# Norming the first two strips of attention probabilities on GpSimd instead of VectorE

## The chip, the cores and the metric

The kernel runs on one core of a Trainium2 chip. The metric is the device time of one execution in microseconds; the time of a kernel is the median of its runs. The profile is of one further execution.

## The reference

Two transformer blocks follow each other on 512 tokens of width 1024, in float32. The first has two attentions, then a gated feed-forward layer; the second has three attentions side by side. What the change touches is the softmax in them:

```python
# block 1, branch A: 8 heads, sliding window of 128, bias and sink column
probs = softmax(concat([logits, sink]))[..., :span];  out = probs @ v
# block 1, branch B: 8 heads; compressed, selected and window attention, gated
p_s = softmax(ls);  p_w = softmax(lw)
out = gate0 * (p_c @ v_cmp) + gate1 * (p_s @ v_slc) + gate2 * (p_w @ v_win)
# block 2: MLA, 8 heads of 96; differential, 4 heads of two maps; memory, 4 heads on 256 keys
p = softmax(causal(q @ k.T * scale));  o = p @ v
a = p[0] - lam * p[1];                 o = a @ v
p = softmax(q @ k_mem.T / 8);          o = p @ v_mem
```

With 512 tokens and 16 blocks of 64 to choose, the selected attention takes all earlier keys, so both it and the window are causal attentions over 512 keys with a bias.

## The kernel before

Matrix products are made in three parts: each operand is split into a rounded part H and a rest L, and `mm3` (L299) adds H x H, H x L and L x H in PSUM. Weights come in 1 MB pieces on SP's queue into one of two buffers `raw`; `wsplit` (L132) rounds a piece to `wH` on ScalarE (L136) and subtracts to `wL` (L137) on VectorE, or on GpSimd where a stage sets `leng` so, as the second attention stage does for its filler.

Attention goes by heads through `pipeline` (L269). A head is a unit with a part a (scores, softmax) and a part b (transposes, product with the values). In step i part a of unit i, part b of unit i-1 and a filler of weight matmuls are woven into one program order; the filler is the dense work that comes next. The planner under the kernel then orders each engine's instructions by that program order and by when it expects their operands; each engine works its own list in order.

Part a treats the 512 queries in four blocks of 128, b = 0 to 3, called strips. A causal strip has 128(b+1) keys, so the strips have 128, 256, 384 and 512 columns; in the sliding window they have 130, 258, 258, 258 (two of them for the sink); in the memory heads each has 256. For each strip TensorE makes the scores in PSUM, `strip` (L482) adds the bias and takes the minimum on VectorE, and ScalarE takes the exponential with its sum (L484). When all four sums are there, VectorE inverts them (in the second stage it also multiplies them by the gate, L950), and each strip is multiplied by its column of inverses, in place in the tile `e` (two buffers): the norming. There are four places for it:

- L677 in `swa_a`, sliding window, 8 heads: all four strips on VectorE.
- L1414 in `scale_strips`, called by `nsa_a` (L951; 8 heads, 2 passes each, selected and window) and by `mla_a` (L1643; 8 heads): strips 0 to 2 on VectorE, strip 3 on ScalarE (L1411, mask `SAN` = `SAM` = 8).
- L1808 in `mem_a`, 4 memory heads: all four strips on VectorE.

The differential heads do not norm; L1733 joins their two maps on VectorE.

Part b transposes the normed 128 x 128 blocks on TensorE in `tr_bank` (L493), up to four into one bank of PSUM; a bank is split to `PTH` on ScalarE (L108) and `PTL` on VectorE (L109) and multiplied with the values. In the causal heads the first bank holds one block of each strip, in the memory heads too; in the sliding window it holds blocks of strips 0, 1 and 2.

GpSimd's other work in these stages: in the sliding window the DMA of each head's bias strip (L647), its sink columns (L648) and the rest of a head's output (L627); in the second stage the bias tile (L941, L942), L627 and the filler's `wL` (L137); around the first MLA heads the rotary embedding of the differential queries and keys (L1190, L1211, L1215, L1217); later the gating of outputs (L1614), the DMAs that rearrange the differential queries (L1692, L1693), and once `yL` (L1843).

Of the kernel before, what the change touches and what calls it, by code (L numbers as in the profile page):

```python
# [66 lines left out]
HPQ = 20  # L67
HPF = 0
PGE = 0.9
SPS = 0  # L70
SPN = 0
SPM = 0
SPE = 0
ZG = 0
DP = 0
BS = 0.25
# [9 lines left out]
class Build:  # L86
# [414 lines left out]
    def block1(self):  # L501
# [140 lines left out]
        def swa_a(h):  # L642
# [27 lines left out]
            for b in range(4):  # L670
# [3 lines left out]
                if SAS >> b & 1:  # L674
                    nc.scalar.activation(es, es, AF.Copy, scale=sm[:, b:b + 1])
                    continue
                (nc.gpsimd if b < SPS else nc.vector).tensor_scalar(es, es, sm[:, b:b + 1], None, op0=ALU.mult)  # L677
            state[h] = blk
# [257 lines left out]
        def nsa_a(h, br):  # L936
# [13 lines left out]
            nc.vector.tensor_tensor(sm, sm, gate[:, :, 3 * h + 1 + br], op=ALU.mult)  # L950
            self.scale_strips(e, sm, SPN, SAN)  # L951
            yield
# [472 lines left out]
    def block2(self, out):  # L1425
# [211 lines left out]
        def mla_a(h):  # L1637
# [4 lines left out]
            v.reciprocal(sm, sm)  # L1642
            self.scale_strips(e, sm, SPM, SAM)  # L1643
            yield
# [144 lines left out]
        def mem_a(h):  # L1789
# [16 lines left out]
            for b in range(4):  # L1806
                es = e[:, 256 * b:256 * b + 256]
                (nc.gpsimd if b < SPE else v).tensor_scalar(es, es, sm[:, b:b + 1], None, op0=ALU.mult)  # L1808
            state["m", h] = e
# [158 lines left out]
```

## Time and profile before

| | |
|---|---|
| median of 3 runs | 1077.21 us (1074.77 to 1085.18) |
| the profiled execution's own time | 1086.88 us, its span 1084.9 us |
| TensorE busy | 1040.1 us, 96% of the span |
| VectorE busy | 751.1 us, 69% |
| ScalarE busy | 581.4 us, 54% |
| GpSimd busy | 233.2 us, 21% |
| sliding window attention | about 80 to 165 us of the span |
| selected and window attention | about 198 to 345 us |
| MLA, then differential and memory heads | about 900 to 972 and 972 to 1045 us |

In the rows PE is TensorE's matmuls, PEld its weight loads, DVE VectorE, ACT ScalarE, POOL GpSimd; L1414 is line 1414 of the kernel. `out<-in` names tiles, `128x256 f32` is partitions by elements. The profile's engine intervals are times in work: waits between instructions are not counted, but an instruction held up while it runs shows a longer duration. The ends of matmuls are modelled. PEclk is the clock granted to TensorE as a share of 2.4 GHz.

### The profile page before, as it was taken

Reading aid. Unit: us, or ns where it says so; the run is one execution under the profiler, and the core shown is the slowest. Engines: PE = TensorE matmul, PEld = TensorE weight load, DVE = VectorE, ACT = ScalarE, POOL = GpSimd, SP = SyncE. Lnnn points to the kernel's source line nnn. Section 1 sums busy time; section 2 is a strip of 40 time slices with the busy share of each in tenths; the row PEclk is TensorE's granted clock in tenths of the full one; section 3 lists DMA queues with packets and bytes.
Section 4 is the critical chain, followed back from the end, with each engine's and each line's share of the span. In section 5 each row is a group of like instructions: output and inputs, shape, how many; then the busy total and the mean of one; then the engine's idle time right before and its main releaser. Section 6 shows DMA issues by size and latency. Waiting matters only on the chain.

```text
span 1084.9 us, 15448 instructions
## 1 busy us (share of the span) xinstructions
PE 1040.1 (96%) x5425; PEld 873.7 (81%) x5425; DVE 751.1 (69%) x1603; ACT 581.4 (54%) x1127; POOL 233.2 (21%) x369
## 2 busy tenths in 40 slices
PE   5899898999999999999999999999999999999898
PEld 3797676878778888888887888887889997877798
DVE  6559885387783275678885468988533497979982
ACT  6447764567784244345553445545643535867630
POOL 4321223322212029000000210000340128230200
PEclk9989998999999999999999999999999999999899
DMA  6936435310233253245669877878855662266442
GB/s 187 278 96 187 107 78 126 83 44 10 45 83 77 72 169 118 78 132 170 205 207 321 289 254 216 256 231 266 292 191 165 226 206 79 79 187 192 141 161 79
DMA packets 131981, 173.09 MB, mean 160 GB/s; under 512 B 8676, under 2 KB 101578, under 8 KB 130752
## 3 DMA queue, kind: packets, MB, share of 16 engines
q1 hardware_dynamic: 127904, 161.47, 48.3%
q0 software_dynamic: 4000, 10.64, 3.2%
q8 instruction: 43, 0.70, 0.3%
q14 instruction: 34, 0.28, 0.1%
HBM read 131.95 MB, written 42.23 MB: 161 GB/s over the span
## 4 chain that ended last, share of the span: by engine, by line
PE 74%; DVE 12%; DMA 6%; ACT 4%; issue 3%; SPq 0%; POOL 0%; POOLq 0%; ACTq 0%; DVEq 0%
PE ps_mm L301 19%; PE ps_mm L306 19%; PE ps_mm L305 18%; DMA raw<-in_w_in 4%; PE ps_S L1361 3%; PE ps_T L493 2%; DVE wL L137 2%; PE ps_O L1390 1%; PE ps_O L1392 1%; DVE PTL L109 1%; PE ps_S L306 1%; PE ps_S L301 1%; PE ps_S L305 1%; ACT wH L136 1%; ACT e L484 1%
## 5 line engine op out<-in xcount | busy, mean ns | idle before, releaser
L136 ACT ACTIVATE wH<-raw 128x1024 fp32r<-128x1024 f32 (+4 forms) x145 | 137.2, 947 | 206.5 <-PE ps_mm L305 159.0
L137 DVE TENSOR_TENSOR wL<-raw,wH 128x1024 fp32r<-128x1024 f32 (+4 forms) x130 | 145.6, 1121 | 98.0 <-ACT wH L136 97.5
L301 PE MATMUL ps_mm<-nH,wH 128*128 128x512 f32 x416 | 162.7, 391 | 0.6 <-DVE qL L115 0.6
L306 PE MATMUL ps_mm<-nH,wL 128*128 128x512 f32 x416 | 162.5, 391 | 0.0
L305 PE MATMUL ps_mm<-nL,wH 128*128 128x512 f32 x416 | 162.4, 390 | 0.0
L484 ACT ACTIVATE e<-e,mn 128x256 f32<-128x256 f32 (+5 forms) x160 | 86.3, 541 | 26.7 <-DVE mn L482 25.5
L301 PE MATMUL ps_mm<-hH,wH 128*128 128x512 f32 x232 | 95.3, 411 | 0.0
L306 PE MATMUL ps_mm<-hH,wL 128*128 128x512 f32 x232 | 92.8, 400 | 0.0
L305 PE MATMUL ps_mm<-hL,wH 128*128 128x512 f32 x232 | 92.7, 400 | 0.0
L301 PEld LDWEIGHTS ps_mm<-nH,wH 128*128 128x128 f32 x416 | 78.1, 188 | 16.6 <-DVE qL L115 0.8
L305 PEld LDWEIGHTS ps_mm<-nL,wH 128*128 128x128 f32 x416 | 78.2, 188 | 15.7
L306 PEld LDWEIGHTS ps_mm<-nH,wL 128*128 128x128 f32 x416 | 78.1, 188 | 15.6
L108 ACT ACTIVATE PTH<-ps_T 128x512 fp32r<-128x512 f32 (+1 forms) x108 | 55.7, 528 | 34.2 <-PE ps_T L493 33.5
L109 DVE TENSOR_TENSOR PTL<-ps_T,PTH 128x512 fp32r<-128x512 f32 (+1 forms) x108 | 63.7, 606 | 12.9 <-ACT PTH L108 10.9
L301 PE MATMUL ps_mm<-aH,wH 128*128 128x512 f32 x176 | 69.6, 396 | 1.1 <-ACT aH L108 1.1
L493 PE MATMUL ps_T<-ident,e 128*128 128x128 f32 x368 | 63.8, 281 | 6.2 <-DVE e L1733 3.1
L305 PE MATMUL ps_mm<-aL,wH 128*128 128x512 f32 x176 | 69.6, 395 | 0.0
L306 PE MATMUL ps_mm<-aH,wL 128*128 128x512 f32 x176 | 69.5, 395 | 0.0
L493 PEld LDWEIGHTS ps_T<-ident,e 128*128 128x128 f32 x368 | 45.6, 143 | 22.6 <-DVE e L1733 4.1
L1075 POOL MEMSET cv<- 128x2 f32 x44 | 4.2, 99 | 236.2 <-DVE cc L1079 229.7
L306 PEld LDWEIGHTS ps_mm<-hH,wL 128*128 128x128 f32 x232 | 44.7, 193 | 9.3 <-DVE wL L137 0.2
L482 DVE CUSTOM_DVE_ANT_0 e<-ps_S,G 128x128 f32<-128x128 f32 (+1 forms) x64 | 30.7, 486 | 29.4 <-PE ps_S L1361 29.0
(585 smaller groups left out, 2624.9 us busy)
## 6 DMA issues: line engine op xcount, KB each, us to landing
raw<-in_w_ffn_in SPq DMA_DIRECT2D x20, 1024.0 KB, 6.1
raw<-in_w_in SPq DMA_DIRECT2D x12, 1024.0 KB, 7.3
pre<-in_w_in SPq DMA_DIRECT2D x17, 512.0 KB, 6.2
raw<-in_w_ffn_out SPq DMA_DIRECT2D x8, 768.0 KB, 5.6
raw<-in_w_ffn_out SPq DMA_DIRECT2D x8, 640.0 KB, 6.1
xt<-in_x SPq DMA_DIRECT2D x8, 512.0 KB, 5.2
raw<-in_w_out SPq DMA_DIRECT2D x4, 1024.0 KB, 5.5
pre_z<-preH SPq DMA_DIRECT2D x16, 256.0 KB, 5.2
```

The source lines that it names most:

```text
L108: nc.scalar.activation(H, src, AF.Copy)
L109: nc.vector.tensor_sub(L, src, f32(H))
L136: self.nc.scalar.activation(H, raw, AF.Copy)
L137: self.leng.tensor_sub(L, raw, f32(H))
L301: ins = mm(ps, wH, xH, start=first, stop=False)
L305: mm(ps, wH, xL, start=False, stop=False)
L306: mm(ps, wL, xH, start=False, stop=last)
L482: nc.vector.tensor_tensor_reduce(e, ps, bias, op0=ALU.add, op1=ALU.min, scale=1.0, scalar=3e38, accum_out=mn)
L484: nc.scalar.activation(e, e, AF.Exp, scale=-1.0, bias=mn, accum_out=sm)
L493: nc.tensor.transpose(ps[:, 128 * i:128 * i + 128], blk, self.ident)
L1361: nc.tensor.matmul(ps[:, :n], q[:, 128 * b:128 * b + 128], k[:, :n], start=i == 0, stop=i == len(prods) - 1)
L1390: mm(out, v2(kb), H[:, c], start=first, stop=False)
```

## The change

`b < SPS` and its like choose GpSimd for strip b; all four limits go from 0 to 2. The multiplications of strips 0 and 1 of every normed head, 72 of them, are then issued on GpSimd, with the same operands. Nothing else is edited.

```diff
-SPS = 0
-SPN = 0
-SPM = 0
-SPE = 0
+SPS = 2
+SPN = 2
+SPM = 2
+SPE = 2
```

The lines that read them (unchanged):

```python
# swa_a
(nc.gpsimd if b < SPS else nc.vector).tensor_scalar(es, es, sm[:, b:b + 1], None, op0=ALU.mult)
# scale_strips(e, sm, pool, sa): pool is SPN in nsa_a, SPM in mla_a
(self.nc.gpsimd if b < pool else self.nc.vector).tensor_scalar(es, es, sm[:, b:b + 1], None, op0=ALU.mult)
# mem_a
(nc.gpsimd if b < SPE else v).tensor_scalar(es, es, sm[:, b:b + 1], None, op0=ALU.mult)
```

## Rows read from the trace of the kernel before

**Rows 1.** The page, busy us by engine (share of the span) and instructions.

```profile
PE 1040.1 (96%) x5425; PEld 873.7 (81%) x5425; DVE 751.1 (69%) x1603; ACT 581.4 (54%) x1127; POOL 233.2 (21%) x369
```

**Rows 2.** Windows of the four stages: length, busy us PE PEld DVE ACT POOL, PEclk, DMA.

```profile
80.00:165.00 85.00, 77.81 (x453) 64.00 (x452) 74.25 (x185) 59.86 (x130) 18.85 (x23) 0.98 0.43 120
198.00:345.00 147.00, 142.57 (x762) 117.34 (x761) 102.92 (x295) 100.17 (x233) 40.35 (x43) 0.99 0.21 50
900.00:972.00 72.00, 67.52 (x398) 56.03 (x397) 59.17 (x153) 52.50 (x127) 34.90 (x55) 0.98 0.34 113
972.00:1045.00 73.00, 68.73 (x408) 58.12 (x407) 67.87 (x183) 48.74 (x140) 12.13 (x9) 0.95 0.50 163
```

**Rows 3.** Timeline, norming runs (start, us); then group of 384 columns (busy, mean ns).

```profile
121.76 1.08 DVE L677 TENSOR_SCALAR e<-e,sm 128x130 f32<-128x130 f32 x4
...
246.61 0.17 DVE L950 TENSOR_TENSOR sm<-sm,gate 128x4 f32<-128x4 f32 x1
246.82 0.88 DVE L1414 TENSOR_SCALAR e<-e,sm 128x128 f32<-128x128 f32 x3
...
1041.56 1.14 DVE L1808 TENSOR_SCALAR e<-e,sm 128x256 f32<-128x256 f32 x4
...
L1414 DVE TENSOR_SCALAR e<-e,sm 128x384 f32<-128x384 f32 x16 | 6.6, 412 | 0.0
```

**Rows 4.** Groups of instructions on GpSimd: busy us, mean ns of one, idle before.

```profile
L1231 POOL TENSOR_SCALAR ang<-inv,pf 128x16 f32<-128x16 f32 x4 | 1.2, 322 | 1.3 <-DVE pf L1227 1.3
...
L1243 POOL TENSOR_SCALAR e<-e 128x768 f32<-128x768 f32 x2 | 4.3, 2134 | 0.2
...
L716 POOL COPY E<-eg 128x16 f32<-128x16 f32 x8 | 1.7, 210 | 18.3 <-DMA eg<-rep 18.3
...
L941 POOL COPY G<-far 128x256 f32<-128x256 f32 x8 | 3.2, 396 | 17.2 <-issue 11.1 <-PE ps_T L493 3.8 <-DVE mn L482 2.1
```

**Rows 5.** Timeline, a VectorE instruction and the GpSimd instruction that waited for it.

```profile
927.50 0.68 DVE L1373 TENSOR_TENSOR y<-ps_O,y 64x512 f32<-64x512 f32 x1
...
928.33 1.27 POOL L1614 TENSOR_TENSOR y<-y,z 64x512 f32<-64x512 f32 x1 [4.61 <-DVE y L1373]
```

**Rows 6.** Timeline, VectorE beside GpSimd; then the group of 128 columns, 198 to 345.

```profile
226.15 2.37 POOL L137 TENSOR_TENSOR wL<-raw,wH 128x1024 fp32r<-128x1024 f32 x1 [11.56 <-ACT wH L136]
...
226.24 2.37 DVE L1414 TENSOR_SCALAR e<-e,sm 128x128 f32<-128x128 f32 x1
...
L1414 DVE TENSOR_SCALAR e<-e,sm 128x128 f32<-128x128 f32 x16 | 9.3, 580 | 0.5
```

**Rows 7.** Timeline, a head's norming on VectorE and the first transposes on TensorE.

```profile
98.81 1.47 DVE L677 TENSOR_SCALAR e<-e,sm 128x130 f32<-128x130 f32 x4
...
100.50 0.55 PE L493 MATMUL ps_T<-ident,e 128*128 128x128 f32 x3
...
322.30 0.88 DVE L1414 TENSOR_SCALAR e<-e,sm 128x128 f32<-128x128 f32 x3
...
323.11 0.45 PE L493 MATMUL ps_T<-ident,e 128*128 128x128 f32 x2
...
1042.79 0.27 PE L493 MATMUL ps_T<-ident,e 128*128 128x128 f32 x1
```

**Rows 8.** Chain that ended last, pieces in the sliding window stage: start, us, what.

```profile
90.61 0.87 DVE e L677 x3
...
122.85 1.23 DVE wL L137
124.09 7.97 DMA raw<-in_w_in
...
161.47 0.62 DVE e L677 x2
```

**Rows 9.** Windows around a stop of TensorE, columns as in group 2.

```profile
229.00:230.40 1.40, 0.70 (x6) 0.69 (x6) 1.40 (x3) 0.04 (x1) 0.01 (x1) 1.00 0.33 31
230.40:233.90 3.50, 3.50 (x10) 2.92 (x9) 3.38 (x13) 1.95 (x6) 0.52 (x1) 0.51 0.91 226
```

## The prediction

> **What bounds the kernel now.** I read the page first, for the share of each engine [rows 1]: TensorE is busy for 96% of the span, VectorE for 69%. An average over stages says little of four short stages, so the second view is the busy time in the windows of the four attentions [rows 2]: sliding window (80 to 165 us), selected and window (198 to 345), MLA (900 to 972), differential with memory (972 to 1045). There the reader is to see two things. TensorE is idle for only 7.2, 4.4, 4.5 and 4.3 us of them, 20.4 of 377. And VectorE is at 87%, 70%, 82% and 93%: it is close to full in the first and in the last stage, not in the second, where half of the moved work lies. GpSimd is at 19 of 85, 40 of 147, 35 of 72 and 12 of 73 us, so it has room. Third come timelines of single heads: when the norming ends and when the first transpose that reads it starts [rows 3, 7].
>
> **What is removed.** One head's norming is a run of VectorE multiplications. A clean head in the second stage has three in 0.88 us, the last of which (384 columns) takes 0.41 [rows 3]; so the two that leave occupied 0.47 us of VectorE's queue. In the sliding window stage and in the memory heads four stand in 1.08 and 1.14 us; I take 0.47 and 0.54 for the first two. With 8 + 24 heads of the first kinds and 4 of memory this is 32 x 0.47 + 4 x 0.54 = 17.2 us of VectorE.
>
> **What is added.** The same 72 multiplications on GpSimd. The trace has no such instruction there with 128 to 258 columns, so I bound its price. Nearest in kind is GpSimd's multiplication by a column of scalars, 16 columns in 322 ns. On the other side of the size stands its addition of a constant, 768 columns in 2134 ns [rows 4]. The line between them rises by 2.41 ns a column and gives 0.59 us for 128 columns and 0.90 for 256: 1.49 us a pair, 1.80 in a memory head. The other end is GpSimd's copy, 210 ns for 16 columns and 396 for 256: 0.69 us a pair. I keep the upper value, since the operation is the same kind as its rows; 0.69 stays for the range. In all about 32 x 1.49 + 4 x 1.80 = 55 us more on GpSimd, which its idle time covers.
>
> The Trainium skill ("GPSIMD Engine Reference", 4.1 Engine selection) calls one-input work on this engine roughly line-rate, which at the 1.2 GHz it gives would be an estimate of 0.32 us of streaming for a pair; the 2.41 ns a column of the rows say otherwise, and the measurement decides.
>
> **What lies on the path.** The transposes of a bank need all strips (in the sliding window stage the first three), so what counts is when the last one is ready. VectorE starts its first multiplication 0.04 us after the scalars are ready; GpSimd started 0.15 us after the VectorE instruction that it waited for [rows 3, 5]. So VectorE's remaining strip goes first. Does GpSimd have to wait for it? The trace shows the two engines excluding each other: a VectorE multiplication of 128 columns, the shortest of a run whose three together take 0.88 us when clean, took 2.37 alone beside a GpSimd subtraction of 2.37 us, and the mean of all 16 in that stage is 0.58 [rows 3, 6]. So I let the pair start when VectorE's strip is done: 0.41 + 1.49 = 1.90 us after the point where VectorE alone needed 0.88. The last strip is 1.02 us later than now; without the exclusion 0.15 + 1.49 against 0.88, 0.76; at the copy's price 0.41 + 0.69 against 0.88, 0.2, about nothing. In a memory head it is 0.61 + 1.80 against 1.14, 1.3 later; for the first bank of a sliding window head about as much.
>
> How much cover is there? I set the end of the norming beside the first transpose for all 36 heads. In 22 the gap is longer than the lateness, or the norming is already held up by other work, and nothing is lost. In 14 it is not: one sliding window head, eight passes of the second stage (among them the last six), four MLA heads and the last memory head. The rows show the first (98.81 + 1.47 = 100.28, transpose at 100.50), one late in the second stage (323.18, 323.11) and the last (1042.70, 1042.79) [rows 3, 7]. Lateness less gap, summed head by head, is 1.1 + 5.4 + 2.7 + 1.2 = 10.4 us that a fixed TensorE order would stand still.
>
> Not all of it reaches the end. The order on each engine is made by the planner from its own costs, and it can put filler matmuls ahead of a transpose that it expects later; but TensorE has only 20.4 us of idle time to absorb the rest. I let two thirds through, 6.9 us.
>
> **What is gained.** VectorE's collisions stay: the strip that is left now meets the same GpSimd instruction that the first one met. What is freed counts where VectorE's queue leads to the next event. The chain that ended last passes through the norming of four of the eight sliding window heads, the first at 90.61, the last at 161.47 us; behind one of them a weight split (1.23 us at 122.85) frees a buffer, and a load of 7.97 us starts [rows 8]. Four times 0.47 is 1.9 us at best. The split reads two SBUF tiles and may meet the new pair, so I take half, 0.9.
>
> **What is queued behind.** On GpSimd stand the bias strip's DMA of the next sliding window head, the subtraction that splits a head's output, the weight splits of the filler in the second stage, the rotary work of the first MLA heads, the gating of MLA and the rearranging DMAs of the differential queries. Each can wait a pair's 1.5 us. The sum counts this at nothing, covered by GpSimd's idle time; if the cover is gone, a weight split is what TensorE needs soonest. No DMA is moved and SP's queue is untouched.
>
> The sum: 6.9 - 0.9 = 6.0 us. The profiled execution took 1086.9 us (span 1084.9 and 2.0 around it), 0.9% over the median of the runs, 1077.2; on the profile's own time that is 1093, on the median 1083.
>
> **Rivals.**
> *VectorE's relief is worth more than the lateness costs* (the other side). For it: 87% and 93% busy in two stages. Against: TensorE is busier. The relief in those two stages is 8 x 0.47 + 4 x 0.54 = 5.9 us, so 1071; if all 17.2 us counted, 1060. It decides if a pair costs no more than the copy's 0.69 us, when nothing comes late.
> *The stops cost TensorE its clock.* After the 1.4 us from 229.0, in which TensorE worked for 0.70, the granted clock was 0.51 of full speed for 3.5 us: the 1.2 GHz level, so 1.7 us lost [rows 9]. With 14 new stops of about a microsecond, all 10.4 us passing through and four such stretches at 1.7, it is 17.2 us: 1094. Against: most stops are shorter than that one.
> *The two engines exclude each other at the new pairs.* If GpSimd gets in first, VectorE's next strip or split stands for the pair. Price: four weight splits of the sliding window stage late by 1.49 - 0.47, 4.1 us, and four memory heads by 1.80 - 0.54, 5.0, where VectorE has 5.1 us of idle time left in all; with the 6.0 above 15.1, so 1092. For it the collision in [rows 6]; against it the 0.15 us by which GpSimd starts later.
> The Trainium skill ("SBUF — State Buffer", Who interferes with whom) states this as an exclusive lock: a VectorE instruction in a two-port mode, or with two SBUF inputs, and a GpSimd instruction reading SBUF block each other whole, whoever comes second. By that rule the trace agrees: 2.37 us for one strip of three that take 0.88.
>
> **How the numbers follow.** My forecast (a few microseconds slower) gets 0.50, the relief 0.15, the clock 0.20, the exclusion 0.15. About 1%, 10.8 us, is what a measurement of this kernel can tell from no change: its three runs lie 10.4 us apart. Of the relief about half lies beyond 1% (0.07 faster); of the clock and the exclusion 0.30, and 0.05 of my forecast's upper tail, lie beyond it on the slow side (0.35); 0.58 stay within. The likeliest case alone spans 1076 to 1089. For 8 in 10 I take in most of the relief below (1068) and both slow rivals (1098).
>
> **What would show it.** Right: GpSimd multiplications of some 0.6 and 0.9 us that start when VectorE's strip ends; new waits of transposes for GpSimd in the late second stage and in MLA, none for VectorE's strips; TensorE's idle time in the four windows up by about 6 us. Wrong: a pair near 0.7 us; transposes that wait no longer than now because other matmuls stand ahead; more stretches at half clock; VectorE's multiplications of 384 columns or its weight splits growing by a GpSimd duration.

## The result and the profile after

The changed kernel takes 1111.33 us (median of 4 runs, 1105.34 to 1113.23), the kernel before beside it 1079.57: a ratio of 1.029 (95% interval 1.026 to 1.032), some 31 us slower. The profiled execution took 1113.23 us with a span of 1111.4, so it is 26.5 us longer than that of before (1084.9). The prediction, 1083 with a range of 1068 to 1098, had the direction of its sum right (+6) and the size wrong by a factor of five.

The page's busy times, to be set beside [rows 1]:

```profile
PE 1044.5 (94%) x5425; PEld 877.5 (79%) x5425; DVE 736.6 (66%) x1531; ACT 582.1 (52%) x1127; POOL 296.9 (27%) x441
```

The 72 instructions have moved. VectorE lost 14.5 us of work (17.2 had been worked out), GpSimd gained 63.7 (55 had been). Neither is anywhere near full.

Windows of the four stages of after, cut so that each holds, to one, as many matmuls as its window in [rows 2] (454, 762, 398, 408); the columns are the same (length, busy us of PE, PEld, DVE, ACT, POOL, PEclk, DMA):

```profile
76.00:170.00 94.00, 80.15 (x454) 67.45 (x453) 73.08 (x170) 59.80 (x130) 37.27 (x47) 0.91 0.43 114
204.50:360.00 155.50, 144.80 (x762) 118.96 (x761) 96.00 (x261) 102.29 (x233) 66.86 (x75) 0.98 0.20 47
914.00:997.50 83.50, 68.10 (x398) 56.75 (x397) 54.57 (x137) 52.58 (x127) 47.93 (x71) 0.92 0.30 97
998.00:1071.80 73.80, 68.81 (x408) 57.55 (x407) 66.71 (x175) 48.06 (x138) 18.38 (x17) 0.95 0.51 164
```

The stages are longer by 9.0, 8.5, 11.5 and 0.8 us, 29.8 in all, of which the span gets 3.3 back elsewhere. TensorE's idle time (length less PE) is 13.9, 10.7, 15.4 and 5.0 us where it was 7.2, 4.4, 4.5 and 4.3: 24.6 us more. The other 5.2 are matmuls that took longer (the clock, below).

What the transposes wait for, from the waits of after (engine, tile and line, releaser: us in total, times, longest):

```profile
PE ps_T L493 <- POOL e L1414: 19.8, 12, 12.6
PE ps_T L493 <- POOL e L677: 7.1, 4, 3.8
```

and from those of before the wait that these replace:

```profile
PE ps_T L493 <- DVE e L1414: 0.9, 3, 0.5
```

These are sixteen waits for strips on GpSimd, 26.9 us together: as much as the span grew. None is for a memory head. But they are not sixteen of a kind: one is 12.6 us, and the two worst in the sliding window stage are 3.8 and 2.2.

**The stop of 12.6 us.** Timeline of after, TensorE and GpSimd around MLA's first head (start, us, engine, line, operation; in brackets the idle time before it and its releaser):

```profile
923.78 0.60 DVE L1414 TENSOR_SCALAR e<-e,sm 128x384 f32<-128x384 f32 x1
...
923.88 0.40 PE L301 MATMUL ps_mm<-nH,wH 128*128 128x512 f32 x1
...
934.90 0.72 POOL L1217 TENSOR_TENSOR dqk<-rt,rt 128x256 f32<-128x256 f32 x1
935.57 0.61 POOL L1675 DMA_DIRECT2D mkl<-mkTl_d  x1
936.23 1.51 POOL L1414 TENSOR_SCALAR e<-e,sm 128x128 f32<-128x128 f32 x2
...
936.90 0.47 PE L493 MATMUL ps_T<-ident,e 128*128 128x128 f32 x1 [12.62 <-POOL e L1414]
```

VectorE has normed its strip of this head at 923.78, so the scalars are there. GpSimd's pair starts 12.45 us later, with no idle time ahead of it: its list has the rotary work of the differential queries and keys first (from 911.73 to 935.6 without a gap) and a DMA behind that. The head's transposes follow the first strip of the pair at once. Before the change the same order was in the trace, and harmless:

```profile
909.91 0.94 DVE L1414 TENSOR_SCALAR e<-e,sm 128x128 f32<-128x128 f32 x2
...
921.11 0.73 POOL L1217 TENSOR_TENSOR dqk<-rt,rt 128x256 f32<-128x256 f32 x1
921.78 0.61 POOL L1675 DMA_DIRECT2D mkl<-mkTl_d  x1
```

From 909.91, when VectorE normed this head, to 922.39, when GpSimd was through with its rotary work, are 12.5 us. Two rows of the old trace give the size of the new stop.

**The stops of the sliding window stage** stand on the chain that ended last (start, us, engine, tile, line); in the old chain the norming steps of this stage were VectorE's [rows 8]:

```profile
76.69 4.58 DMA eg<-rep
...
82.34 0.72 POOL ast L647
83.27 1.52 POOL e L677 x2
84.83 0.91 PE ps_T L493 x3
...
111.32 2.15 POOL X L757
113.47 3.27 POOL e L677 x2
116.78 0.90 PE ps_T L493 x3
```

Head 0's pair stands behind a copy that waits for a DMA (76.69, 4.58 us), behind the copies after it and behind the issue of the next bias strip: again the queue in front of the pair, not the pair. Head 3's pair stands behind a two-input subtraction of 2.15 us, but it also took 3.27 us itself where head 0's took 1.52. Timeline of after, head 3:

```profile
111.15 2.92 DVE L677 TENSOR_SCALAR e<-e,sm 128x258 f32<-128x258 f32 x2
...
114.26 0.33 PE L493 MATMUL ps_T<-ident,e 128*128 128x128 f32 x1 [0.70 <-POOL e L677]
...
114.80 1.21 DVE L137 TENSOR_TENSOR wL<-raw,wH 128x1024 fp32r<-128x1024 f32 x1
...
116.78 0.90 PE L493 MATMUL ps_T<-ident,e 128*128 128x128 f32 x3 [2.19 <-POOL e L677]
```

The first strip of the pair cost TensorE 0.70 us, the second 2.19: that one ran beside a weight split on VectorE, which has two tiles as input (114.80, 1.21 us), and was held. VectorE's own two strips of this head (2.92 us) had been held by the subtraction before. So head 3's stop is in part the two engines hindering each other, and not the queue alone.

**The clock.** From 928.8, within the long stop, to 942.5 the granted clock is at half, the 1.2 GHz level. Shorter stops have their stretch too, at 82.3 (stop of 3.8 us) and at 328.0 (1.3 us). Windows of after:

```profile
82.30:89.10 6.80, 4.74 (x21) 4.45 (x22) 2.70 (x6) 2.71 (x7) 2.47 (x5) 0.50 0.34 92
328.00:331.40 3.40, 3.40 (x14) 2.90 (x12) 2.47 (x6) 1.79 (x4) 0.00 (x0) 0.51 0.00 0
928.80:942.50 13.70, 5.60 (x23) 5.36 (x24) 2.65 (x8) 2.65 (x7) 8.50 (x15) 0.50 0.11 38
```

All stretches at half clock hold 37.2 us of TensorE's work in after and 28.5 in before, so 8.7 us more of it ran at half speed: an estimate of 4.4 us, which is also what TensorE's busy time grew by from page to page (1040.1 to 1044.5). But the profile of before is of an execution of 1086.88 us with a granted clock of 0.985, and the medians of before are 1077 to 1080. A kernel below whose time is level with before (e4, an execution of 1078.83 us at 0.992) has this page:

```profile
PE 1036.0 (96%) x5425; PEld 869.3 (81%) x5425; DVE 749.8 (70%) x1595; ACT 580.7 (54%) x1127; POOL 242.3 (22%) x377
```

Against it the same 5425 matmuls took 8.5 us more in after. So of the 31 us between the medians some 9 are the clock's by this estimate, and the rest is TensorE standing still.

### The profile page after: what moved, and what is told of

Read it like the earlier page. It is cut to its first block, busy times and chain, and to the rows that moved or that the text cites. A ratio compares the mean times of both kernels' runs of the same rounds, so it can differ in the third digit from the quotient of the medians.

```text
span 1111.4 us, 15484 instructions
## 1 busy us (share of the span) xinstructions
PE 1044.5 (94%) x5425; PEld 877.5 (79%) x5425; DVE 736.6 (66%) x1531; ACT 582.1 (52%) x1127; POOL 296.9 (27%) x441
## 4 chain that ended last, share of the span: by engine, by line
PE 67%; DVE 12%; DMA 7%; POOL 6%; ACT 4%; issue 3%; SPq 0%; POOLq 0%; ACTq 0%; DVEq 0%
PE ps_mm L301 17%; PE ps_mm L305 17%; PE ps_mm L306 17%; PE ps_T L493 3%; PE ps_S L1361 3%; DMA eg<-rep 2%; DMA raw<-in_w_in 2%; POOL e L1414 1%; PE ps_O L1390 1%; PE ps_O L1392 1%; DVE wL L137 1%; DMA rep<-rvec 1%; ACT wH L136 1%; DMA raw<-in_cmp_w_v 1%; ACT e L484 1%
## 5 line engine op out<-in xcount | busy, mean ns | idle before, releaser
L493 PE MATMUL ps_T<-ident,e 128*128 128x128 f32 x368 | 67.3, 293 | 32.7 <-POOL e L1414 19.8
L109 DVE TENSOR_TENSOR PTL<-ps_T,PTH 128x512 fp32r<-128x512 f32 (+1 forms) x108 | 63.7, 606 | 15.6 <-ACT PTH L108 15.3
L1414 POOL TENSOR_SCALAR e<-e,sm 128x128 f32<-128x128 f32 (+1 forms) x48 | 40.0, 843 | 69.8 <-DVE sm L950 24.7
```

The lines of the kernel that those rows point to most:

```text
L109: nc.vector.tensor_sub(L, src, f32(H))
L493: nc.tensor.transpose(ps[:, 128 * i:128 * i + 128], blk, self.ident)
L1414: (self.nc.gpsimd if b < pool else self.nc.vector).tensor_scalar(es, es, sm[:, b:b + 1], None, op0=ALU.mult)
```

## The theories and the experiments

*Lateness*: each pair is late by its own length against VectorE's strips, and many small waits add up; that is the prediction's sum, with its factor wrong. *Queue*: a few pairs stand in GpSimd's list behind work that has nothing to do with their head, and these few stops are most of the loss. *Planner*: 72 moved instructions make the planner order the whole program another way, and the loss can't be laid to a stage. Each kernel below was timed beside the kernel before on its chip (medians of 1079 to 1080 us), and its ratio is to that; "us over before" is the ratio's excess over 1 times that median.

**One stage at a time.** Four kernels, each with one of the four limits at 2 and the rest at 0:

```diff
-SPS = 0
+SPS = 2
```

> Only the sliding window heads are normed in two strips on GpSimd. Queue theory (the pair stands in GpSimd's queue behind other work, at head 0 behind a copy that waits 4.1 us for its DMA, at head 3 behind a 2.15 us subtraction): TensorE's matmuls wait about 7 us for GpSimd's strips in this stage as in the changed kernel, and the time is 5 to 8 us over before. Lateness theory (each pair is simply 1 us late, with the small gaps counted before): +1 us, at most +2. Planner theory (a new order of instructions costs wherever it falls): the loss does not sit at transposes that wait for GpSimd, and the stages behind differ too.

> Only the selected and window attention is normed in two strips on GpSimd. Lateness theory: +3.6 to +5.4 us (the sum of lateness less gap, two thirds or all of it). Queue theory: +6 to +9 us, with the longest waits of transposes for GpSimd where the pair starts behind a weight split. Planner theory: another number than the 8 us that this stage grew by in the changed kernel, with the loss outside the transposes' waits.

> Only the MLA heads are normed in two strips on GpSimd. Queue theory: the first head's pair stands behind the whole rotary work of the differential queries and keys, TensorE stops for about 13 us once and runs at half clock behind it: +13 to +16 us. Lateness theory: +1.8 to +2.7 us. Planner theory: the stop may vanish with another order, anything from 0 to +16.

> Only the memory heads are normed in two strips on GpSimd. Queue theory: GpSimd is nearly free here, 0 +- 2 us. Lateness theory: +0.8 to +1.2 us. Relief theory (VectorE is at 93% here): -2 us. If the four parts add up to the 32 us of the whole change, the stages act on their own; if they don't, the order of the whole matters.

| kernel | median us | ratio (95%) | us over before |
|---|---|---|---|
| e1, sliding window only | 1092.11 | 1.0104 (1.0078 to 1.0130) | 11.2 |
| e2, second stage only | 1086.12 | 1.0057 (1.0040 to 1.0074) | 6.2 |
| e3, MLA only | 1093.37 | 1.0138 (1.0102 to 1.0174) | 14.9 |
| e4, memory heads only | 1080.40 | 1.0016 (0.9994 to 1.0038) | 1.7 |

The four add up to 3.15%, the whole change costs 2.9%: within the intervals the stages are independent, and no loss is left that only a new order of the whole program would bring. That speaks against the planner theory. e3 and e4 came out as the queue theory had it. e1 lies above its 5 to 8 us, and e2 above the lateness theory's 3.6 to 5.4, at the low end of the queue theory's 6 to 9. The loss does not go by the moved work either: the second stage has 32 of the 72 instructions and 6.2 us, MLA has 16 and 14.9. In e3 the same stop stands alone, here in its timeline:

```profile
920.60 1.51 POOL L1414 TENSOR_SCALAR e<-e,sm 128x128 f32<-128x128 f32 x2
921.27 0.48 PE L493 MATMUL ps_T<-ident,e 128*128 128x128 f32 x1 [12.60 <-POOL e L1414]
```

**Sliding window without its two queued heads.** Heads 0 and 3 norm on VectorE, the other six as changed:

```diff
-(nc.gpsimd if b < SPS else nc.vector).tensor_scalar(
+(nc.gpsimd if b < SPS and h not in (0, 3) else nc.vector).tensor_scalar(
```

> As the run with the sliding window heads alone on GpSimd (+11 us), but heads 0 and 3 stay on VectorE: those whose pairs stood behind a copy waiting for its DMA and behind a 2.15 us subtraction. Queue theory: the four waits of 7.2 us vanish, and the half clock behind them: +1 to +4 us over before. Lateness theory: the other six heads keep most of the loss, +6 to +9. Planner theory: the loss stays near +11 or jumps.

1083.18 us, ratio 1.0034 (1.0012 to 1.0056): 3.7 us over before where e1 had 11.2. No transpose waits for L677 on GpSimd any more. Two heads of eight carried 7.5 us of 11.2; for head 3 that is the queue and the hold by the weight split together. Where the remaining 3.7 arise, with no such wait left, these runs do not settle; the granted clock of its executions, 0.990 in the mean against 0.993 beside it, goes the same way.

**One strip instead of two in the second stage** (`SPN = 1`), so that GpSimd's part of a head is some 0.6 us and VectorE's two strips take about as long:

> In the selected and window attention only strip 0 (128 columns) goes to GpSimd. It starts 0.15 us later and takes 0.74 beside VectorE, so it ends about when VectorE's last strip ends: nothing is late. Lateness theory: 0 to +1 us (two strips: +6). Queue theory: +2 to +4, where the strip stands behind a weight split. Planner theory: any number, +6 as likely as 0.

1081.02 us, ratio 1.0003 (0.9985 to 1.0022). The waits of e2 and then of this kernel:

```profile
PE ps_T L493 <- POOL e L1414: 6.7, 9, 1.3
```

```profile
PE ps_T L493 <- POOL e L1414: 1.7, 2, 1.1
```

Nine waits of at most 1.3 us and 6.2 us of time go together, two waits and nothing go together. In this stage the loss is lateness in the main. Two of the five passes that wait in e2 have something else in it: one pair starts 0.9 us after its scalars, behind other work of GpSimd, and of one the second strip is held beside a weight split on VectorE (the wait of 1.3 us).

**The rotary work kept in its place.** First as a control, with all strips on VectorE: the multiplication on GpSimd with which each block of the rotary work starts (L1190) is held to the order in which the program has it, so that the block can't be drawn ahead of the MLA heads (operands cut to `...`).

```diff
-(eng or nc.vector).tensor_tensor(t[:, b], t[:, b], ..., op=ALU.mult)
+ins = (eng or nc.vector).tensor_tensor(t[:, b], t[:, b], ..., op=ALU.mult)
+ins = self.tc.keep_in_program_order(ins) if eng is not None else ins
```

> The kernel before, with the rotary work of the differential queries and keys kept at its place in the program order on GpSimd instead of floating ahead; the other engines' orders are the same. A control for the next run: 0 +- 3 us by every theory; a loss would say that the differential heads need that work early.

1081.57 us, ratio 1.0019 (0.9992 to 1.0045): the edit by itself is not told from nothing. Then the same with `SPM = 2`:

> As the control, with the MLA heads normed in two strips on GpSimd. The first head's pair now stands ahead of the rotary work on GpSimd's queue. Queue theory: the stop of 12.6 us goes, +1 to +4 us over the control instead of +15. Lateness theory alone: +2 to +3 as well. Against the queue: if the stop stays although the pair stands first, or the loss is over +10, the order of the queue is not its cause.

1087.14 us, ratio 1.0064 (1.0043 to 1.0084): 6.9 us over before where e3 had 14.9, some 5 over its control (1 to 4 had been expected). The waits of e3 and of e8:

```profile
PE ps_T L493 <- POOL e L1414: 13.1, 3, 12.6
```

```profile
PE ps_T L493 <- POOL e L1414: 4.4, 7, 1.6
```

With the rotary work in its place the long stop is gone, and seven short waits are left. Not all of them are lateness. Timeline of e8, its longest:

```profile
937.55 0.62 POOL L1675 DMA_DIRECT2D mkl<-mkTl_d  x1
938.21 1.50 POOL L1414 TENSOR_SCALAR e<-e,sm 128x128 f32<-128x128 f32 x2
...
938.88 0.33 PE L493 MATMUL ps_T<-ident,e 128*128 128x128 f32 x1 [1.58 <-POOL e L1414]
```

This pair starts 2.8 us after its scalars, and another (919.24) 2.4 us after its own, both behind rotary work that program order itself puts there. These two pairs make 3.2 of the 4.4 us.

**Both causes, crossed.** Three kernels complete a square with the changed one: one or two strips per head in all four attentions, with the queue as it comes or cured (heads 0 and 3 of the sliding window on VectorE, the rotary work in place).

> One strip per head on GpSimd in all four attentions, nothing else altered. Queue theory (the strips stand behind other work in GpSimd's queue, and that is most of the loss): the stops of 12.6 us in MLA and of 4 us and 3.3 us in swa stay, so the time is 18 to 24 us over the kernel before (about 1097 to 1103 us), with some 20 us of matmul waits for GpSimd's strips. Lateness theory (the second strip comes too late, and that is the loss): with the pair halved to 0.6 to 0.74 us the scalars-to-strip time falls under what VectorE's own strips take, and the time is within 5 us of the kernel before, with under 5 us of such waits.

> One strip per head on GpSimd in all four attentions, heads 0 and 3 of swa left on VectorE, and the rotary work's place in GpSimd's queue kept in program order. Queue theory and lateness theory together: both causes are gone, so the time is 0 to 4 us over the kernel before (1079 to 1083 us), with under 4 us of matmul waits for GpSimd's strips. If there is a third cause that grows with GpSimd's load as such, it is 8 us or more over. If VectorE's relief is worth something once nothing waits, it is up to 5 us below the kernel before.

> Two strips per head on GpSimd in all four attentions as in the change, heads 0 and 3 of swa left on VectorE, and the rotary work kept in program order. Queue theory: the 12.6 us stop and the swa stops are gone and what is left is the lateness of the pairs; the sum of the single runs (3.7 swa, 6.2 nsa, 6.9 MLA, 1.7 memory) is 18 us over the kernel before, about 1097 us, so 14 us less than the changed kernel, with 12 to 16 us of matmul waits for GpSimd's strips. Lateness theory alone: the queue's order doesn't matter and the time stays within 4 us of the changed kernel, 1108 us or more.

| us over before (ratio, 95%) | queue as it comes | queue cured |
|---|---|---|
| two strips | 31 (1.029, 1.026 to 1.032) | 16.2 (1.0150, 1.0122 to 1.0178) |
| one strip | 21.0 (1.0195, 1.0154 to 1.0236) | 3.0 (1.0028, 1.0003 to 1.0053) |

Curing the queue is worth 15 us with two strips and 18 with one; leaving one strip is worth 10 and 13. By the intervals each of these is good to some 5 us. So about half of the loss is the queue, about a third to two fifths the lateness of the second strip, and 3 us is what is left of both. The border between the two is not sharp: the cure takes the hold of head 3's second strip along, and it leaves two MLA pairs behind rotary work (3.2 us of waits in e11, as in e8). In each share the clock that follows the stops is included. The halved pair does not help against the queue; timeline of e9, one strip, nothing cured:

```profile
915.27 0.62 POOL L1414 TENSOR_SCALAR e<-e,sm 128x128 f32<-128x128 f32 x1
...
915.95 0.47 PE L493 MATMUL ps_T<-ident,e 128*128 128x128 f32 x1 [12.70 <-POOL e L1414]
```

Waits of e10 (one strip, cured), then of e11 (two, cured):

```profile
PE ps_T L493 <- POOL e L1414: 6.5, 6, 2.6
```

```profile
PE ps_T L493 <- POOL e L1414: 11.1, 16, 1.6
```

e11 has sixteen waits again, as many as the changed kernel, but the longest is 1.6 us, and their sum is a little under the forecast 12 to 16. Two more things did not come as expected. The sliding window stops were not in e9's profile (one wait of 0.7 us), while its time was as forecast; that profile is of an execution of 1092.95 us, and others took up to 1104.11, so where those lost more is not shown. And e10's waits, 6.5 us, are over the forecast 4: a transpose at 939.36 waited 2.6 us for a strip that still stood behind rotary work, one at 920.44 1.5 us.

**One head of 36.** The changed kernel with MLA's first head back on VectorE:

```diff
-self.scale_strips(e, sm, SPM, SAM)
+self.scale_strips(e, sm, SPM if h else 0, SAM)
```

> The changed kernel with one head out of 36 altered: MLA's first head norms its strips 0 and 1 on VectorE again. Queue theory: that pair is where the 12.6 us stop stood, behind the rotary work in GpSimd's queue. Head 0 no longer waits; head 1's pair, some 9 us behind it, may still meet the end of the rotary work for about 2 us. So the time falls by 8 to 12 us against the changed kernel, to about 1100 us (1099 to 1103). Lateness theory: one head of 36 is worth about a microsecond, so the time stays at 1109 to 1112 us.

1106.26 us (1093.17 to 1109.75), ratio 1.0216 (1.0147 to 1.0284): by the ratios 8 us under the changed kernel, but the interval reaches into that one's, and the median lies over the forecast 1099 to 1103, so the time alone decides nothing. Its waits, in the profile of the execution of 1109.75 us:

```profile
PE ps_T L493 <- POOL e L1414: 12.5, 13, 4.9
```

The stop did not go, it moved: head 1's pair, whose scalars came while the rotary work still ran, now makes TensorE wait for 4.9 us (2 had been expected). From the first matmul of line 1629 to the first of line 1821 the stage takes 93.0 us, where the changed kernel took 100.0 and the kernel before 87.7.

## Why the prediction was wrong

**What failed: "What is queued behind".** The step listed GpSimd's other work, the rotary work of the first MLA heads and the bias strip's DMA among it, asked who stands behind a pair, and "counts this at nothing, covered by GpSimd's idle time". The pairs stand behind that work as well. Idle time on average is no cover for an instruction that needs the engine within 2 us: GpSimd was busy for 35 of MLA's 72 us [rows 2], and 12.5 of these 35 came without a gap right after head 0's norming began. This term was 0 and measured 15 to 18 us, with the clock that follows such stops and the hold at head 3 in it. [rows 7] set every head's norming beside its transposes; what was never set beside them was GpSimd's own list at that moment.

**The prices were near.** The groups of after on GpSimd (busy us, mean ns), to be set beside the bounds of [rows 4]:

```profile
L1414 POOL TENSOR_SCALAR e<-e,sm 128x256 f32<-128x256 f32 x24 | 23.2, 967 | 0.0
L1414 POOL TENSOR_SCALAR e<-e,sm 128x128 f32<-128x128 f32 x24 | 17.2, 718 | 69.8 <-DVE sm L950 24.7 <-DVE sm L1642 24.1 <-PE ps_O L963 12.7
...
L1808 POOL TENSOR_SCALAR e<-e,sm 128x256 f32<-128x256 f32 x8 | 7.5, 954 | 14.2 <-DVE sm L1805 7.9 <-DVE ro L384 6.3
```

They are 0.72 and 0.97 us in the mean against 0.59 and 0.90; the pair at 936.23, with nothing beside it on VectorE, took 1.51 against 1.49. The line between the two rows of the same kind held, the copy's price did not. The rule that the prediction quoted from the Trainium skill ("GPSIMD Engine Reference", 4.1 Engine selection), one-input work at roughly line rate, does not fit these rows: its estimate of 0.32 us, for streaming alone, stands against a pair of 1.51, almost five times.

**The lateness: near in size, for a wrong reason and with luck, and mis-sized in what it costs.** Timeline of after, a head of the second stage:

```profile
253.77 0.17 DVE L950 TENSOR_TENSOR sm<-sm,gate 128x4 f32<-128x4 f32 x1
...
254.13 1.52 POOL L1414 TENSOR_SCALAR e<-e,sm 128x128 f32<-128x128 f32 x2 [4.89 <-DVE sm L950]
254.99 0.41 DVE L1414 TENSOR_SCALAR e<-e,sm 128x384 f32<-128x384 f32 x1
```

The last strip is ready 1.71 us after the scalars (253.94 to 255.65); 1.90 had been worked out, with the pair waiting for VectorE's strip. It doesn't wait: it starts 0.19 us after the scalars. The gross of the waits, 10.4 us, is near what the kernel with the queue cured shows (11.1), but that is partly luck. The second stage had 5.4 in it, and e2 shows 6.7; MLA had 2.7, and e8 shows 4.4, most of it behind rotary work; the sliding window and the memory heads had 2.3, and e11 shows no wait there. The step that let only two thirds through, for filler that the planner would put ahead, failed: e11 loses 16 us with 11.1 us of such waits, e2 6.2 with 6.7. TensorE stands still for all of it. What e11 loses beyond its waits, some 5 us, is found in the matmuls: TensorE's busy time is 1040.5 us on its page, at a granted clock of 0.986, against the 1036.0 of e4 at 0.992.

**No gain.** 14.5 us less work on VectorE brought nothing that a run shows; even e6, with 1.7 us of waits left, is level with the kernel before and not below it, and no kernel here was faster. The old chain passed through the norming of four sliding window heads on VectorE; the new one has one such step (0.84 us at 141.63) and, shown above, GpSimd's pairs of heads 0 and 3 with 1.52 and 3.27 us. The relief rival falls with that.

**The clock rival** had its mechanism and nearly its size: four stretches at 1.7 us made 6.8, and 4.4 us are measured against the one profile of before, some 9 against a level kernel. It is the stops' companion, not the loss itself; the stretch at the long stop, with 5.6 us of work in it, is the largest, and short stops have theirs. What was wrong in its 1094 were the stops that it started from.

**The exclusion rival** did not decide: the two engines' strips hardly hinder each other (below). Where a strip of VectorE met a two-input instruction of GpSimd it was held as in [rows 6], now with GpSimd's pair queued behind the same instruction. The price came the other way round: GpSimd's strips were held by VectorE's weight splits, where the rival had splits held by the pair. Two such holds made TensorE wait, 2.19 us at head 3 and 1.30 in the second stage; strips not held cost 0.43 and 0.57 there, so an estimate of 2.5 us.

**The range** ended at 1098, a little beyond the dearest rival (1094). No rival had a pair that waits on its own engine's list, although the text names the rotary work. The 12.5 us of the two rows of before, on top of the sum's 6.0, would have made one of 1077.2 + 18.5 = 1096 from a single head; with the lateness passed through whole (10.4 for 6.9) it is 1099, and with the 7.5 us that e5 found in two sliding window heads 1107.

## What to carry to other kernels

When an instruction is moved to an engine with room, read that engine's list at the moments when the instruction will be due: what stands in front of it there, from the time its operand is ready to the time the engine is through, is the stop that the move can bring, and an average busy share doesn't show it. Such a list can also stand still: at head 0 a copy that waited 4.1 us for its DMA held up the pair behind it. Work that a planner has drawn ahead on an idle engine costs nothing until something urgent is put on that engine. Price and queue are two terms, and halving the first (one strip for two) leaves the second whole.

## What was unexpected of the hardware

[rows 6] had suggested that VectorE and GpSimd exclude each other at such strips. Timeline of after, first two normings of MLA heads, then one of the second stage beside a weight split on GpSimd:

```profile
945.12 0.42 DVE L1414 TENSOR_SCALAR e<-e,sm 128x384 f32<-128x384 f32 x1
945.18 1.73 POOL L1414 TENSOR_SCALAR e<-e,sm 128x128 f32<-128x128 f32 x2 [7.44 <-DVE sm L1642]
...
959.98 1.60 POOL L1414 TENSOR_SCALAR e<-e,sm 128x128 f32<-128x128 f32 x2 [4.39 <-DVE sm L1642]
960.38 0.42 DVE L1414 TENSOR_SCALAR e<-e,sm 128x384 f32<-128x384 f32 x1
...
299.30 1.29 POOL L137 TENSOR_TENSOR wL<-raw,wH 128x512 fp32r<-128x512 f32 x1 [4.46 <-ACT wH L136]
299.41 1.39 DVE L1414 TENSOR_SCALAR e<-e,sm 128x384 f32<-128x384 f32 x1
```

Beside GpSimd's multiplication, which has one tile as input, VectorE's strip takes 0.42 us, as when alone (0.41 [rows 3]), whichever came first; GpSimd's pair takes 1.60 to 1.73 instead of 1.51. Strips of 256 columns are slowed a little more: the group of the memory heads (L1808) takes 0.41 us in the mean, 0.35 before. Beside GpSimd's subtraction, which has two, the same strip takes 1.39. The Trainium skill ("SBUF — State Buffer", Who interferes with whom) states that a VectorE instruction in a two-port mode and a GpSimd instruction block each other whole. The rows agree for GpSimd's two-input instruction and differ for its one-input multiplication; the measurement decides. What in the one-input instruction lets VectorE through was not tried.
